# The second branch gate of a hybrid decoder layer as seven half-size products instead of eight projections

## Chip, cores and metric

The kernel runs on 1 core of one Trainium2 chip. The metric is the time of one execution of the whole program on the device, in microseconds (us). Each matrix product is made in fp32r: both operands are split into a high and a low part (`h`, `l`), and a product is three matrix multiplications, h·h + l·h + h·l.

## What is computed

One decoder layer on 512 tokens of 1024 features, in float32:

```python
u = rms_norm(x, g)
z = u @ w_in        # q, k, v | conv q, k | v | output gate | i, f | gate A | gate B
A = moba_attention(...)             # 8 heads of 64
B = mlstm_chunkwise(...)            # 4 heads of 128
merged = sigmoid(ga) * (ya @ w_proj_a) + sigmoid(gb) * (yb @ w_proj_b)
h = x + merged @ w_out
h = h + (silu(g) * up) @ w_down     # g, up = rms_norm(h) @ w_gate_up
return rms_norm(h, norm_final_g)
```

The change is about `gb`, the second branch gate: a product of 512 x 1024 by 1024 x 1024.

## The kernel before

**Units.** The work up to the output projection is a list of weight units (`UNITS`), in the order in which TensorE takes them: q, k, va, ob, vb, qkb, ob, then ga 0 to 7, gb 0 to 7, p 0 to 7 (both branch projections of one block of 128 features) and wo 0 to 7. A unit is 128 x 1024 numbers of weights (512 KB). `load_pair` queues its load on SyncE (SP) into a `raw` tile of the R pool (9 tiles). `split_unit` makes `wh` on ScalarE (ACT) and `wl` on VectorE (DVE), in two tiles of the W pool (10 tiles). The split activations `uh`, `ul` of four feature blocks lie in tiles of these two pools (two in each, named `u` in the trace) until the last unit that reads them, so that 8 tiles of W, four units, are left to the weights. `fill` takes the next unit: it makes the splits up to `LOOK` units ahead, calls `make_sums`, and runs the unit's matrix multiplications.

**Gates.** A unit of ga or gb (`proj`, `run_g`) is 24 matrix multiplications of 128 x 128 by 128 x 512 into one PSUM tile `mm` (there are three): the weights are stationary, the 512 tokens move past. ga is copied out by ACT and scaled by the row `rb` (1/rms of each token) later, in `gate`; gb is scaled by `rb` when DVE moves it out (line 561). `gate(m)` takes the sigmoids; `run_p` multiplies them with the two projections and splits the sum (`mgh`, `mgl`) for wo.

**Steps.** Attention heads and mLSTM heads go through a list of steps; each step calls `fill(1)` once, so that a unit lies between the small products of the heads. In the mLSTM steps each head needs its decay rows `R` (`ml_load`, line 1603: a load of 896 KB on the POOL queue out of `scr`), masked on DVE (line 1615) and taken to Exp on ACT. `ml_d1` and `ml_d2` normalise a head, `ml_e` applies its output gate.

**Sums.** The FFN uses products of sums of weight blocks. `sum_steps` makes these sums (`ws`) in device memory: a copy on the SP queue, then an accumulating DMA on the POOL queue. `make_sums` issues them one by one and lets each wait for a matrix multiplication of the unit before, so that they are spread; they are held back in steps 12 to 20.

**Order.** Each engine and each DMA queue runs its instructions in the order in which they stand. A scheduler makes that order from the program's order and its priorities, within the limits of the pools.

Of the kernel before, what the change touches and what calls it, by code (L numbers as in the profile page):

```python
# [15 lines left out]
P = 128  # L16
# [35 lines left out]

def _unit_order():
# [10 lines left out]
    u += [("gb", m) for m in range(8)]  # L64
    u += [("p", m) for m in range(8)]
# [5 lines left out]
NGEN = len(UNITS)  # L71

# [21 lines left out]
def hybrid_layer_kernel(ctx: ExitStack, tc, xT, wall, wgc, wgu, wds, wdl, g3v, vecs, wgates, consts, rope, out):  # L94
# [71 lines left out]
    def split_hl(src, name="h", dst=None):  # L166

        h, l = dst or (slot(F32R, name + "h"), slot(F32R, name + "l"))
        act_(h, src, AF.Copy)
        V.tensor_tensor(l, src, f(h), op=ALU.subtract)  # L170
        return h, l

# [16 lines left out]
    def load_pair():  # L189
        p = wstate["pair"]  # L190
        if p * 2 >= NU:
            return
        for u in (2 * p, 2 * p + 1):
            raw[u] = blk(name="raw", raw=True)
            nc.sync.dma_start(raw[u], wall[u])
        wstate["pair"] += 1
# [8 lines left out]
    def mm3(ps, wh, wl, wk, rh, rl, start, stop):  # L205

        n = len(wk)
        for j, k in enumerate(wk):
            c = slice(k * P, (k + 1) * P)
            st["mm"] = T.matmul(ps, wh[:, c], rh[j], start=start and j == 0, stop=False)  # L210
            T.matmul(ps, wl[:, c], rh[j], start=False, stop=False)  # L211
# [22 lines left out]
    for k in range(KT):  # L234
        for j in (0, 2) if k == 0 else (0,):
            c = slice(j * P, (j + 2) * P if k == 0 else S)
            nc.sync.dma_start(t0[k // 4][:, k % 4, c], wall[k // 2, :, (k % 2) * S : (k % 2 + 1) * S][:, c])
            if k:
                nc.sync.dma_start(xs[k], xT[k])
    wstate["pair"] = 2  # L240
    wstate["split"] = 4
# [91 lines left out]
    def newton(r, v, new):  # L333
# [3 lines left out]
        V.scalar_tensor_tensor(t, t, -0.5, v, op0=ALU.mult, op1=ALU.mult)  # L337
# [41 lines left out]
    def fill(n=1, mid=None):  # L379

        for _ in range(n):
# [9 lines left out]
            kind, i = UNITS[u]  # L391
# [16 lines left out]
    st = {"made": 0, "hold": False}  # L408
# [156 lines left out]
    for kd in ("ob", "ga", "gb"):  # L565
        run[kd] = run_g(kd)


    mgd = []

    def gate(m):
# [3 lines left out]
        act_(ga, ga, AF.Sigmoid)  # L575
        act_(gb, gb, AF.Sigmoid)

    def run_p(m, wh, wl):
        if m == 0:
            gate(0)  # L580
        if m >= 4:
            load_xr()
        pa, pb = mmb(), mmb()
        mm3(pa, wh, wl, range(4), [t[0] for t in ya], [t[1] for t in ya], True, True)
        mm3(pb, wh, wl, range(4, 8), [t[0] for t in yb], [t[1] for t in yb], True, True)
        yield
        ga, gb = gz.pop(("ga", m)), gz.pop(("gb", m))
        V.tensor_tensor(ga, pa, ga, op=ALU.mult)
        V.tensor_tensor(gb, pb, gb, op=ALU.mult)
        if m < KT - 1:  # L590
            gate(m + 1)
        V.tensor_tensor(ga, ga, gb, op=ALU.add)
        mgd.append(split_hl(ga, "mg"))
# [63 lines left out]
    def run_wo(i, wh, wl):  # L657
# [3 lines left out]
        mm3(ps, wh, wl, range(8), [t[0] for t in mgd], [t[1] for t in mgd], True, True)  # L661
# [54 lines left out]
    def sum_steps():  # L716

        def made(key, *terms):
            t = sums[key] = dram.tile(list(terms[0].shape), F32, name=nm("ws"))
            yield nc.sync.dma_start(t, terms[0], max_dma_last_dim=8192)  # L720
            for x in terms[1:]:
                yield nc.gpsimd.dma_start(t, x, accum_op=ALU.add, max_dma_last_dim=8192)

        for c in range(NG):
            w = wgc[c]
            g = lambda k: sums["gc", c, k]
            yield from made(("gc", c, "S1"), w[0], w[1])
            yield from made(("gc", c, "S3"), w[0], w[2])
            w = wds[c]
            g = lambda k: sums["ds", c, k]  # L730
            yield from made(("ds", c, "S1"), w[1], w[2])
            yield from made(("ds", c, "S3"), w[0], w[1])
# [25 lines left out]
    making = sum_steps()  # L758
# [1112 lines left out]
```

## Time and profile before

| | |
|---|---|
| median of 3 runs | 715.16 us (714.8 to 715.38) |
| the profiled execution | 715.64 us, its span 713.6 us |
| granted TensorE clock, mean of the span | 0.997 |
| PE instructions | 3272 |
| DVE busy, instructions | 600.0 us, 986 |
| ACT busy, instructions | 438.0 us, 746 |
| DMA | 152.69 MB, mean 214 GB/s |

The span runs from the first instruction to the last; 2.04 us of the execution lie around it. The eight units of gb are the ones before the first product of the attention branch's projection (ya), which starts 300.10 us into the span. Where times are given as "at 233 us", they count from the start of the span.

### The profile page before, as it was taken

Reading aid. Unit: us, or ns where it says so; the run is one execution under the profiler, and the core shown is the slowest. Engines: PE = TensorE matmul, PEld = TensorE weight load, DVE = VectorE, ACT = ScalarE, POOL = GpSimd, SP = SyncE. Lnnn points to the kernel's source line nnn. Section 1 sums busy time; section 2 is a strip of 40 time slices with the busy share of each in tenths; the row PEclk is TensorE's granted clock in tenths of the full one; section 3 lists DMA queues with packets and bytes.
Section 4 is the critical chain, followed back from the end, with each engine's and each line's share of the span. In section 5 each row is a group of like instructions: output and inputs, shape, how many; then the busy total and the mean of one; then the engine's idle time right before and its main releaser. Section 6 shows DMA issues by size and latency. Waiting matters only on the chain.

```text
span 713.6 us, 9515 instructions
## 1 busy us (share of the span) xinstructions
PE 703.6 (99%) x3272; PEld 585.8 (82%) x3272; DVE 600.0 (84%) x986; ACT 438.0 (61%) x746; POOL 69.8 (10%) x97
## 2 busy tenths in 40 slices
PE   9999999999999999999999999999999999999995
PEld 6888888887888888888888888888888888888884
DVE  6788977888998578666699887898999799797996
ACT  6634888668784446723354756566675666575665
POOL 0013010000001000000020110011002004003000
PEclk9999999999999999999999999999999999999998
DMA  9759685623159997989988667669569649869703
GB/s 326 290 189 242 207 219 173 199 78 151 60 204 244 277 297 218 275 258 269 265 253 198 218 196 216 233 178 302 198 187 278 226 136 220 312 158 272 217 0 119
DMA packets 47009, 152.69 MB, mean 214 GB/s; under 512 B 5837, under 2 KB 6229, under 8 KB 42481
## 3 DMA queue, kind: packets, MB, share of 16 engines
q1 hardware_dynamic: 36880, 117.33, 47.7%
q0 software_dynamic: 9792, 34.21, 23.5%
q8 instruction: 26, 0.43, 0.2%
q10 hardware_dynamic: 288, 0.56, 0.2%
q14 instruction: 23, 0.18, 0.1%
HBM read 130.00 MB, written 53.52 MB: 257 GB/s over the span
## 4 chain that ended last, share of the span: by engine, by line
PE 82%; DVE 12%; ACT 3%; issue 2%; DVEq 0%; ACTq 0%
PE mm L212 10%; PE mm L210 10%; PE mm L211 10%; PE mm L855 5%; PE mm L856 5%; PE mm L854 5%; PE s L855 3%; PE s L856 3%; PE s L854 3%; PE mm L1104 2%; PE mm L1102 2%; PE mm L1101 2%; PE mm L315 2%; PE acc L315 2%; PE acc L856 1%
## 5 line engine op out<-in xcount | busy, mean ns | idle before, releaser
L157 ACT ACTIVATE w<-raw 128x1024 fp32r<-128x1024 f32 (+2 forms) x107 | 108.1, 1023 | 47.7 <-PE mm L855 20.0
L829 DVE TENSOR_TENSOR w<-raw,w 128x1024 fp32r<-128x1024 f32 x70 | 84.4, 1219 | 21.3 <-ACT w L157 21.0
L157 ACT ACTIVATE wh<-raw 128x1024 fp32r<-128x1024 f32 x56 | 59.0, 1054 | 61.4 <-PE mm L211 58.7
L170 DVE TENSOR_TENSOR wl<-raw,wh 128x1024 fp32r<-128x1024 f32 x56 | 68.2, 1218 | 10.2 <-ACT wh L157 10.0
L854 PE MATMUL mm<-w,bq 128*128 128x512 f32 x160 | 62.2, 389 | 0.0
L855 PE MATMUL mm<-w,bq 128*128 128x512 f32 x160 | 62.2, 389 | 0.0
L856 PE MATMUL mm<-w,bq 128*128 128x512 f32 x160 | 62.2, 389 | 0.0
L210 PE MATMUL mm<-u,wh 128*128 128x512 f32 x128 | 50.3, 393 | 0.0
L211 PE MATMUL mm<-u,wl 128*128 128x512 f32 x128 | 50.0, 391 | 0.0
L212 PE MATMUL mm<-u,wh 128*128 128x512 f32 x128 | 50.0, 390 | 0.0
L212 PE MATMUL mm<-ul,wh 128*128 128x512 f32 x128 | 49.8, 389 | 0.0
L211 PE MATMUL mm<-uh,wl 128*128 128x512 f32 x128 | 49.8, 389 | 0.0
L210 PE MATMUL mm<-uh,wh 128*128 128x512 f32 x128 | 49.8, 389 | 0.0
L854 PEld LDWEIGHTS mm<-w,bq 128*128 128x128 f32 x160 | 30.0, 188 | 6.3
L855 PEld LDWEIGHTS mm<-w,bq 128*128 128x128 f32 x160 | 30.0, 188 | 6.3
L856 PEld LDWEIGHTS mm<-w,bq 128*128 128x128 f32 x160 | 30.0, 188 | 6.2
L1010 DVE TENSOR_TENSOR w<-raw,w 128x1024 fp32r<-128x1024 f32 x25 | 30.2, 1216 | 1.4 <-ACT w L157 1.0
L1102 PE MATMUL mm<-w,ac 128*128 128x512 f32 x80 | 31.2, 389 | 0.0
L1101 PE MATMUL mm<-w,ac 128*128 128x512 f32 x80 | 31.1, 389 | 0.0
L854 PE MATMUL s<-w,bq 128*128 128x512 f32 x80 | 31.1, 389 | 0.0
L855 PE MATMUL s<-w,bq 128*128 128x512 f32 x80 | 31.1, 389 | 0.0
L856 PE MATMUL s<-w,bq 128*128 128x512 f32 x80 | 31.1, 389 | 0.0
(438 smaller groups left out, 1917.1 us busy)
## 6 DMA issues: line engine op xcount, KB each, us to landing
raw<-in_wall_dram SPq DMA_DIRECT2D x56, 512.0 KB, 5.6
raw<-in_wgc_dram SPq DMA_DIRECT2D x30, 512.0 KB, 5.1
raw<-ws SPq DMA_DIRECT2D x30, 512.0 KB, 5.8
ws<-in_wgc_dram SPq DMA_DIRECT2D x10, 1024.0 KB, 6.9
ws<-in_wgc_dram POOLq DMA_DIRECT2D x10, 1024.0 KB, 9.3
raw<-in_wds_dram SPq DMA_DIRECT2D x15, 512.0 KB, 6.6
ws<-in_wds_dram SPq DMA_DIRECT2D x10, 512.0 KB, 7.3
ws<-in_wds_dram POOLq DMA_DIRECT2D x10, 512.0 KB, 6.7
```

Source lines behind the costliest of these rows:

```text
L157: return A.activation(out_, in_, func, **kw)
L170: V.tensor_tensor(l, src, f(h), op=ALU.subtract)
L210: st["mm"] = T.matmul(ps, wh[:, c], rh[j], start=start and j == 0, stop=False)
L211: T.matmul(ps, wl[:, c], rh[j], start=False, stop=False)
L212: T.matmul(ps, wh[:, c], rl[j], start=False, stop=stop and j == n - 1)
L829: V.tensor_tensor(l, t, f(h), op=ALU.subtract)
L854: st["mm"] = T.matmul(ps[t], bh, wh[:, d], start=first and k == 0, stop=False, skip_group_check=not first)
L855: T.matmul(ps[t], bh, wl[:, d], start=False, stop=False, skip_group_check=not first)
L856: T.matmul(ps[t], bl, wh[:, d], start=False, stop=k == 3, skip_group_check=not first)
L1010: V.tensor_tensor(w[k][1], g[k], f(w[k][0]), op=ALU.subtract)
L1101: T.matmul(ps, bh, wh[:, d], start=first and k == 0, stop=False, skip_group_check=not first)
L1102: T.matmul(ps, bl, wh[:, d], start=False, stop=False, skip_group_check=not first)
```

## The change

The gate gb is made as one group `gs` of 14 units (seven weight blocks of 512 x 512, two units each) by a scheme of seven products of half-size blocks in place of eight. The operands change places: the 128 tokens of a block of `u` are stationary and 512 output features move, 12 matrix multiplications of 128 x 128 by 128 x 512 in a unit.

- Four of the seven weight blocks are sums (S1, S2, S3, S4). They are made in device memory as the FFN's sums are, ahead of these: `sum_steps` begins with them, from step 1 of the list that `make_sums` works off; the steps are paced anew by the unit's number, no longer held back in steps 12 to 20, and none is issued during gs.
- The token side needs sums as well. `load_x` loads x anew, in two tiles of 1 MB (`cA`, `cB`) on the POOL queue, and `combine` makes four blocks of them on ACT and DVE (rows of 128 x 256). `recast` splits each block into the half of `uh[0..3]`, `ul[0..3]` that the group before has finished with, 16 splits of 128 x 256.
- The results stand with tokens on the partitions. ACT and DVE move them out and scale them by a token's column (`rt`, `nrt`), DVE turns blocks of 32 x 32 (8 transposes), four DMAs write each half to device memory (`gd`) and four read it back (`gb`), on the POOL queue.
- The projections run in the order 4 to 7, 0 to 3 (`PORD`). The first two leave PSUM by four ACT copies (`pa`, `pb`), and `gate` stands behind these copies; the tiles of gb come in another order of tokens, so that `merge` reads the projection and writes the product with turned access patterns.
- The copy `nsb` of `ml_d1` goes from DVE to ACT, and the scaling by 2^-39 in `ml_d2` goes into the ACT instruction and `newton`, four DVE instructions less.

```diff
+GW = ("W11", "S1", "S2", "W12", "S3", "S4", "W22")
+PORD = (4, 5, 6, 7, 0, 1, 2, 3)
...
-    u += [("gb", m) for m in range(8)]
-    u += [("p", m) for m in range(8)]
+    u += [("gs", i) for i in range(2 * len(GW))]
+    u += [("p", m) for m in PORD]
...
+            if kind == "gs":
+                w, j = GW[i // 2], slice(i % 2 * D, i % 2 * D + D)
+                src = sums["gs", w] if w[0] == "S" else wgb[{"W11": 2, "W12": 3, "W22": 1}[w]]
+                nc.sync.dma_start(raw[u], src[:, j])
...
-            while wstate["split"] <= min(u + LOOK, NGEN - 1):
+            while wstate["split"] <= min(u + LOOK + (kind == "gs"), NGEN - 1):
                 split_unit()
             pos[0] += 1
-            make_sums(st["made"] if st["hold"] else min(st["made"] + 2, 6 * (u - 17) // 7))
+            v = u if u < G0 else max(u + G0, 2 * u - 2 * len(GW)) // 2
+            make_sums(5 * (min(v, G0) - 19 + max(v - G0 - 10, 0)) // 4)
...
+    def load_x():
+        for n, c in (("A", slice(0, 4)), ("B", slice(4, 8))):
+            gs[n] = slot4(name="c" + n)
+            nc.gpsimd.dma_start(gs[n], xT[c].rearrange("k p s -> p k s"))
+        yield
+
+    def combine():
+        for k in range(4):
+            x, v = gs["A"][:, k], gs["B"][:, k]
+            ng = ng1[:, k : k + 1]
+            with tc.issue_after(raw_ins(last["a"])), tc.issue_after(raw_ins(last["v"])):
+                act_(v, v, AF.Copy, scale=col(G1 + k + 4))
+                V.tensor_tensor(x[:, A_], x[:, A_], x[:, B_], op=ALU.subtract)
+            V.scalar_tensor_tensor(x[:, B_], x[:, B_], ng, v[:, B_], op0=ALU.mult, op1=ALU.add)
+            V.scalar_tensor_tensor(v[:, B_], x[:, A_], ng, v[:, B_], op0=ALU.mult, op1=ALU.subtract)
+            V.scalar_tensor_tensor(v[:, A_], v[:, B_], -1.0, v[:, A_], op0=ALU.mult, op1=ALU.subtract)
+            yield
...
+    def run_gs(i, wh, wl):
...
+        for t in range(2):
+            for e in range(2):
+                k = 2 * j + e
+                q = lambda u: u[k0 + k][:, HS * half + P * t : HS * half + P * t + P]
+                c = slice(e * S, (e + 1) * S)
+                g = dict(skip_group_check=not first)
+                st["mm"] = T.matmul(ps[t], q(uh), wh[:, c], start=first and k == 0, stop=False, **g)
+                T.matmul(ps[t], q(uh), wl[:, c], start=False, stop=False, **g)
+                st["gs"] = T.matmul(ps[t], q(ul), wh[:, c], start=False, stop=k == 3, **g)
+        yield
+        if j == 0:
+            if w in ("W11", "S1", "S2", "W12"):
+                recast(w)
+            return
...
+            V.transpose(gs["t", n][:, :, 2 * h + t, :], o.rearrange("p (b e) -> p b e", e=32))
+        if w in ("S4", "W22"):
...
+            for m in range(4):
+                z = gz["gb", 4 * n + m] = slot(name="gb")
+                nc.gpsimd.dma_start(z, d[m * P : (m + 1) * P, :])
...
-        act_(ga, ga, AF.Sigmoid)
-        act_(gb, gb, AF.Sigmoid)
+        with tc.issue_after(raw_ins(last["g"])):
+            act_(ga, ga, AF.Sigmoid)
+            act_(gb, gb, AF.Sigmoid)
...
+        if m in PORD[:2]:
+            q = slot(name="pa"), slot(name="pb")
+            for t, z in zip((pa, pb), q):
+                last["g"] = act_(z, t, AF.Copy)
...
-        V.tensor_copy(nsb, num)
+        act_(nsb, num, AF.Copy)
...
-        V.tensor_scalar(d2, d2, 2.0**-39, None, op0=ALU.mult)
...
-        17: [ml_w(1)], 18: [silu_batch([2, 6, 3, 7])], 19: [ml_w(3)],
+        17: [ml_w(1)], 18: [silu_batch([2, 6, 3, 7])], 19: [ml_w(3)], 20: [load_x()], 25: [combine()],
...
-        st["hold"] = 12 <= n <= 20
```

The order moves in two places of which the prediction speaks. On DVE, before, near the end of the gate; `gb<-mm` moves a finished unit out of PSUM, `wl` is the low part of a weight unit, `nt` and `yb` belong to the mLSTM heads:

```order
L1698 SCALAR_TENSOR_TENSOR nt_2730<-nt_2730,vec,ob_1035 128x512
L170 TENSOR_TENSOR wl_2982<-raw_2814,wh_2981 128x1024
L170 TENSOR_TENSOR yb_2941<-nt_2618,yb_2941 128x512
L561 TENSOR_TENSOR gb_2975<-mm_2950,vec 128x512
L170 TENSOR_TENSOR yb_2941<-nt_2730,yb_2941 128x512
L1698 SCALAR_TENSOR_TENSOR nt_2885<-nt_2885,vec,ob_2120 128x512
L170 TENSOR_TENSOR wl_3024<-raw_2907,wh_3023 128x1024
```

On DVE, now, near the end of gs; `u` is the low part of a recast block, `gW` and `gS` are results on their way out, `gt` the turned ones, and `wl_3101` is the low part of the last unit of gs:

```order
L1852 SCALAR_TENSOR_TENSOR nt_2914<-nt_2914,vec,ob_2247 128x512
L175 TENSOR_TENSOR wl_3039<-raw_2949,wh_3038 128x1024
L658 SCALAR_TENSOR_TENSOR gW_2861<-acc_3011,rt,gW_2861 128x512
L175 TENSOR_TENSOR yb_3000<-nt_2914,yb_3000 128x512
L659 STREAM_TRANSPOSE gt_3054<-gW_2861 128x16x32
L658 SCALAR_TENSOR_TENSOR gW_2863<-acc_3012,rt,gW_2863 128x512
L175 TENSOR_TENSOR wl_3060<-raw_2951,wh_3059 128x1024
L659 STREAM_TRANSPOSE gt_3054<-gW_2863 128x16x32
L175 TENSOR_TENSOR wl_3080<-raw_3007,wh_3079 128x1024
L658 SCALAR_TENSOR_TENSOR gS_2935<-mm_2793,nrt,gS_2935 128x512
L658 SCALAR_TENSOR_TENSOR gS_2937<-mm_2794,nrt,gS_2937 128x512
L659 STREAM_TRANSPOSE gt_3095<-gS_2935 128x16x32
```

Weight units stand twice as close to each other for the same matrix work, and results and transposes stand between them. From the low part of the first unit of the gate to that of the last, DVE had 54 instructions before (8 of 1024 columns, 45 of 512, 1 of 384) and has 98 now (14 of 1024, 50 of 512, 2 of 384, 32 of 256).

On the POOL queue, before, around the decay rows `R`; `ws` are the sums' adding transfers:

```order
L1603 DMA R_1756<-scr 128x1792
L722 DMA ws_1486<-in_wgc_dram 128x2048
L1603 DMA R_2050<-scr 128x1792
L1603 DMA R_2114<-scr 128x1792
L1603 DMA R_2281<-scr 128x1792
L722 DMA ws_2388<-in_wgc_dram 128x2048
L722 DMA ws_2465<-in_wds_dram 64x2048
```

And now, with the gate's sums (`in_wgb`) and x (`cA`, `cB`):

```order
L848 DMA ws_1923<-in_wgb_dram 128x2048
L848 DMA ws_1835<-in_wgc_dram 128x2048
L848 DMA ws_2206<-in_wgb_dram 128x2048
L1758 DMA R_2300<-scr 128x1792
L848 DMA ws_2031<-in_wgc_dram 128x2048
L590 DMA cA_2377<-in_xT_dram 128x4x512
L848 DMA ws_2271<-in_wds_dram 64x2048
L590 DMA cB_2379<-in_xT_dram 128x4x512
L848 DMA ws_2487<-in_wds_dram 64x2048
```

The last head's decay rows now stand behind three adding transfers of 1 MB and ahead of both tiles of x, and `cB` behind one of 0.5 MB more.

More of the change, by code (lines that the diff above doesn't have):

```diff
@@ L71 @@
 NGEN = len(UNITS)
+G0 = UNITS.index(("gs", 0))
 NG = 5
@@ L239, in hybrid_layer_kernel @@
                 nc.sync.dma_start(xs[k], xT[k])
+    wstate["split"] = 4
     wstate["pair"] = 2
-    wstate["split"] = 4
     load_pair()
@@ L406, in proj @@
         return ps
-    st = {"made": 0, "hold": False}
+    st = {"made": 0}
     def run_qk(kind):
@@ L563, in run_g @@
         return fn
-    for kd in ("ob", "ga", "gb"):
+    for kd in ("ob", "ga"):
         run[kd] = run_g(kd)
-    mgd = []
+    A_, B_ = slice(0, HS), slice(HS, S)
+    gs = {}
+    def load_x():
[14 more added lines that the diff above has]
+            yield
@@ L571, in gate @@
+    run["gs"] = run_gs
+    mgd = {}
     def gate(m):
@@ L584, in run_p @@
         mm3(pa, wh, wl, range(4), [t[0] for t in ya], [t[1] for t in ya], True, True)
+        if m == PORD[0]:
+            tc.add_manual_dep(raw_ins(st["first"]), raw_ins(st["gs"]).name, behind, reason="order")
         mm3(pb, wh, wl, range(4, 8), [t[0] for t in yb], [t[1] for t in yb], True, True)
         yield
[L587 to L593, printed above, removed]
+        if m in PORD[:2]:
+            q = slot(name="pa"), slot(name="pb")
+            for t, z in zip((pa, pb), q):
+                last["g"] = act_(z, t, AF.Copy)
+            early.append((m, *q))
+            if m == PORD[1]:
+                gate(PORD[0])
+                for x in early:
+                    merge(*x)
+        else:
+            merge(m, pa, pb)
     run["p"] = run_p
@@ L660, in run_wo @@
         ps = mmb()
-        mm3(ps, wh, wl, range(8), [t[0] for t in mgd], [t[1] for t in mgd], True, True)
+        mm3(ps, wh, wl, range(8), [mgd[k][0] for k in range(KT)], [mgd[k][1] for k in range(KT)], True, True)
         residual()
@@ L716, in sum_steps, with copied, added, groups @@
     def sum_steps():
[L718 to L732, printed above, removed]
+        def copied(a):
+            t = dram.tile(list(a.shape), F32, name=nm("ws"))
+            return t, nc.sync.dma_start(t, a, max_dma_last_dim=8192)
+        def added(key, t, b):
+            i = nc.gpsimd.dma_start(t, b, accum_op=ALU.add, max_dma_last_dim=8192)
+            sums[key] = t
+            return i
+        def groups():
+            prev = None
+            for c in range(NG):
+                w, v = wgc[c], wds[c]
+                for key, a, b in (
+                    (("gc", c, "S1"), w[0], w[1]), (("gc", c, "S3"), w[0], w[2]),
+                    (("ds", c, "S1"), v[1], v[2]), (("ds", c, "S3"), v[0], v[1]),
+                ):
+                    t, i = copied(a)
+                    yield i
+                    if prev:
+                        yield added(*prev)
+                    prev = key, t, b
+            yield added(*prev)
+        rest = groups()
+        s1, i = copied(wgb[0])
+        yield i
+        s3, i = copied(wgb[0])
+        yield i
+        yield added(("gs", "S1"), s1, wgb[1])
+        yield added(("gs", "S3"), s3, wgb[2])
+        yield next(rest)
+        s2, i = copied(s1)
+        yield i
+        yield next(rest)
+        yield added(("gs", "S2"), s2, wgb[2])
+        yield next(rest)
+        s4, i = copied(s2)
+        yield i
+        yield next(rest)
+        yield added(("gs", "S4"), s4, wgb[3])
+        yield from rest
     sums = {}
@@ L1415, in hybrid_layer_kernel @@
     columns(rb[0:1, :], rt.rearrange("p (j h) -> p j h", h=1))
+    ng1 = cst.tile([P, 4], F32, name="ng1")
+    V.tensor_scalar(ng1, vec[:, G1 : G1 + 4], -1.0, None, op0=ALU.mult)
+    nrt = cst.tile([P, 4], F32, name="nrt")
+    V.tensor_scalar(nrt, rt, -1.0, None, op0=ALU.mult)
     man.close()
```

97 lines of the change are left out of this document (78 added, 19 removed).

## The prediction, made before the result was known

> **What bounds the kernel now.** I read the page's busy times first, then PE's waits, then the stretch of the gate engine by engine. The busy times:
>
> ```profile
> PE 703.6 (99%) x3272; PEld 585.8 (82%) x3272; DVE 600.0 (84%) x986; ACT 438.0 (61%) x746; POOL 69.8 (10%) x97
> ```
>
> A busy PE can hide waits, so the view of waits for PE alone decides:
>
> ```profile
> PE s L1571 <- ACT P L162: 1.0, 2, 0.7
> PE s L231 <- DVE mask L219: 1.0, 1, 1.0
> PE acc L1021 <- DVE w L799: 0.6, 1, 0.6
> ```
>
> In the whole span PE waits 2.6 us for others, and nowhere near the gate. PE is the bound from end to end: a matrix multiplication less is time less, and a wait made on PE is time more, one for one. What a multiplication costs is the distance between two starts, not its duration of 0.39. The timeline of PE, first and last row of 90 unbroken ones and the row after:
>
> ```profile
> 279.70 0.39 PE L210 MATMUL mm<-u,wh 128*128 128x512 f32 x1
> ...
> 299.88 0.39 PE L212 MATMUL mm<-ul,wh 128*128 128x512 f32 x1
> 300.10 0.39 PE L210 MATMUL mm<-ya,wh 128*128 128x512 f32 x1
> ```
>
> (300.10 - 279.70) / 90 = 0.2267 us. A unit of ga or gb (24) takes 5.44, one of gs (12) 2.72.
>
> How full are the others there? Windows from the first split of the gate's weights to its end (columns: PE, PEld, DVE, ACT, POOL, clock, DMA share, GB/s):
>
> ```profile
> 233.00:255.00 22.00, 22.00 (x103) 18.38 (x102) 14.64 (x22) 10.75 (x18) 1.62 (x2) 1.00 0.96 269
> 255.00:292.00 37.00, 37.00 (x168) 30.66 (x167) 29.28 (x43) 23.90 (x38) 3.18 (x4) 1.00 0.87 244
> ```
>
> DVE works 43.9 us of 59, ACT 34.7, and the DMA engines are nearly full. The room that the change needs is on DVE and in the DMA.
>
> **Part 1: fewer multiplications.** gb has 8 x 24 = 192, gs 14 x 12 = 168, all of 512 columns, and no other count changes: 24 x 0.2267 = 5.44 us less on the path. This term is certain as long as PE isn't made to wait.
>
> **Part 2: DVE in the gate's stretch.** The distances between starts on DVE, for the widths that matter:
>
> ```profile
> 214.75 1.21 DVE L170 TENSOR_TENSOR wl<-raw,wh 128x1024 fp32r<-128x1024 f32 x1
> 215.88 0.41 DVE L1645 TENSOR_TENSOR R<-R 128x256 f32<-128x256 f32 x1
> 216.22 0.68 DVE L170 TENSOR_TENSOR ya<-ya,ya 128x512 fp32r<-128x512 f32 x1
> 216.82 0.28 DVE L1646 TENSOR_TENSOR R<-R 128x128 f32<-128x128 f32 x1
> 217.02 0.55 DVE L170 TENSOR_TENSOR Al<-R,Ah 128x384 fp32r<-128x384 f32 x1
> 217.49 0.68 DVE L170 TENSOR_TENSOR ya<-ya,ya 128x512 fp32r<-128x512 f32 x1
> ```
>
> 1.13 us for 1024 columns, 0.34 for 256, 0.60 for 512, 0.47 for 384. The transposes I count as 512 columns: the kernel has eight of that size later, a tenth of a microsecond longer at most.
>
> ```profile
> L648 DVE STREAM_TRANSPOSE ht<-xr 128x512 f32<-128x512 f32 x8 | 5.6, 704 | 0.0
> ```
>
> From the first weight unit's low part to the last one's, the 98 instructions of the changed order make 14 x 1.13 + 50 x 0.60 + 2 x 0.47 + 32 x 0.34 = 57.6 us; the 54 of before made 36.5. When may they start? The first split waits for a place in the W pool, four units back, and the places are as many as before:
>
> ```profile
> 232.28 1.06 ACT L157 ACTIVATE wh<-raw 128x1024 fp32r<-128x1024 f32 x1 [5.16 <-PE mm L211]
> 233.38 1.23 DVE L170 TENSOR_TENSOR wl<-raw,wh 128x1024 fp32r<-128x1024 f32 x1 [3.09 <-ACT wh L157]
> ```
>
> So DVE starts at 233.38 and, never idle, ends the last low part at 291.0. Without a stall PE ends gs at 300.10 - 5.44 = 294.66 and starts its last unit at 291.94; that unit's first two products need only the high part, so the low part is due at 292.4. The margin is 1.4 us for everything that DVE waits for in 58. Two kinds of waits come.
>
> (a) x. `combine` stands from the third DVE instruction on, at about 235.6, and needs `cB` and two ACT copies of it (0.5 us each and the hand-over: 1.5). The two tiles go on the POOL queue, among the sums' adds. Its transfers, KB each and median us to landing:
>
> ```profile
> ws<-in_wgc_dram POOLq DMA_DIRECT2D x10, 1024.0 KB, 9.3
> ws<-in_wds_dram POOLq DMA_DIRECT2D x10, 512.0 KB, 6.7
> R<-scr POOLq DMA_DIRECT2D x4, 896.0 KB, 6.2
> h1d<-ht POOLq DMA_DIRECT2D x8, 256.0 KB, 6.1
> ```
>
> The add ahead of `cA` is paced by the second unit of ga, the one ahead of `cB` by the third. The first products of these two on PE before:
>
> ```profile
> 204.26 0.39 PE L210 MATMUL mm<-u,wh 128*128 128x512 f32 x1
> ...
> 211.60 0.44 PE L210 MATMUL mm<-u,wh 128*128 128x512 f32 x1
> ```
>
> 5.44 later, at 209.7 and 217.0, the adds may go. Wholly overlapped, `cB` lands 9.3 after its own issue at about 217.5: 226.8. Wholly one after the other it lands at 209.7 + 9.3 + 9.3 + 6.7 + 9.3 = 244.3. With a DMA share of 0.96 there I take a little past the middle, 236: DVE goes on at 237.5, 1.9 us idle. The Trainium skill would have it otherwise ("DMA: Bandwidth & Descriptors", Anatomy of one DMA): some 2 us and the bytes at 436 GB/s, 4.4 us for 1 MB by its fit; by that the tile is there by 222, this wait is nothing, and the sum below gains 1.9. The rows of this queue (9.3) speak against it in this crowd.
>
> (b) hand-overs. Recast, gates and mLSTM tails go from ACT to DVE and back; such a hop costs about 0.2 us where nothing covers it (0.18 in the row below). I count seven that follow a PE or ACT release late in the order: 1.4.
>
> ```profile
> 267.59 1.23 DVE L170 TENSOR_TENSOR wl<-raw,wh 128x1024 fp32r<-128x1024 f32 x1 [0.18 <-ACT wh L157]
> ```
>
> 1.9 + 1.4 - 1.4 = 1.9 us that PE waits for the low parts of the last units of gs. Bounds: nothing, if `cB` comes before 234; 10, if it comes at 244 (236 gives 1.9, and each microsecond later one more).
>
> **Part 3: ACT, and what is queued behind its waits.** From start to start a split takes 0.95 us there, 512 columns take 0.52 to 0.60:
>
> ```profile
> 204.38 1.05 ACT L157 ACTIVATE wh<-raw 128x1024 fp32r<-128x1024 f32 x1
> 205.33 0.57 ACT L157 ACTIVATE ga<-mm 128x512 f32<-128x512 f32 x1
> 205.93 0.60 ACT L157 ACTIVATE yl<-acc 64x512 f32<-64x512 f32 x1
> ...
> 285.35 0.62 ACT L162 ACTIVATE ga<-ga 128x512 f32<-128x512 f32 x1
> 285.87 0.62 ACT L162 ACTIVATE gb<-gb 128x512 f32<-128x512 f32 x1
> ```
>
> It gains 6 splits, 16 recasts of 256 columns (an estimate of 0.3 each, half of 0.6), 4 copies of x, 6 results and 4 `nsb` (0.55 each): 18 us, together 53 of 59, so it doesn't bind by its sum. But the copies of `cB` stand ahead of the copy that frees the fourth ga unit's PSUM, which the seventh wants at about 240.6: PE is hit there directly if `cB` comes after 238. At 236 it costs nothing. Likewise the last decay rows:
>
> ```profile
> 209.95 1.14 DVE L1615 SCALAR_TENSOR_TENSOR R<-con,cS,R 128x128 f32<-128x128 f32 x4 [0.90 <-DMA R<-scr]
> ```
>
> DVE waits 0.9 us for them already. Now up to one more add of 9.3 us lies ahead of them; I take 3 us, which the 3.09 us of idle time in the row at 233.38 swallows. If that cover is gone it adds to (a).
>
> **Part 4: the way back of gb.** The first half is complete when S4 has left PE, 5.44 us ahead of the end of gs. DVE evacuates and turns it behind low parts that are due first (about 6 us after PE), the four stores take 0.68 x 3 + 6.1 = 8.1 (issues follow each other at 0.68, row below), the loads 5 to 7 (the 256 KB row above), then a sigmoid, three more ACT instructions and a sum on DVE, 4.4, until the third projection's first product leaves PSUM.
>
> ```profile
> 367.85 2.66 POOL L652 DMA_DIRECT2D h1d<-ht  x4 [6.90 <-DVE v L687]
> ```
>
> 6 + 8.1 + 6 + 4.4 = 24.5. PE wants that PSUM tile 5.44 + 3 x 5.44 + 2.72 = 24.5 us after S4. It is a tie, which part 2's delay of PE loosens a little; I take 0.5 (0 to 3). The second half has 10 us more. ACT stands with the sigmoid until then; the weight splits behind it are four units early, so only this PSUM tile counts.
>
> **Nothing else on the path.** The sums' 8 MB run mostly between 125 and 214, and the loads of gs are seven units early. The DMA engines' busy tenths, 40 slices of 17.8 us:
>
> ```profile
> DMA  9759685623159997989988667669569649869703
> ```
>
> Slices 8 to 12, from 125 on, are 6, 2, 3, 1 and 5: there is room. `nsb` and the four scalings are counted above. For wo the last projection now comes fourth of eight, not last. How long its way out of PSUM and its split take, from the seventh of before, which leaves PE at 300.10 + 7 x 5.44 = 338.2:
>
> ```profile
> 338.38 0.69 DVE L589 TENSOR_TENSOR gb<-mm,gb 128x512 f32<-128x512 f32 x1 [1.69 <-PE mm L212]
> ...
> 340.85 0.68 DVE L170 TENSOR_TENSOR mgl<-ga,mgh 128x512 fp32r<-128x512 f32 x1
> ```
>
> 3.3 us to the end of the low part. The order puts five products of the next unit ahead of the one that needs it, and reaches that after 15 products, 3.4 us; 0.1. FFN, tail and start keep their order but for pacing.
>
> **Sum.** -5.44 + 1.9 + 0.5 + 0.1 = -2.9 us. The profiled execution took 715.64 (span 713.6 and 2.04 around it), which makes 712.7; against the median of the runs, 715.16, it is 712.2. That is 0.4% faster. 0.2% (1.43 us) is about what a measurement of this kernel can tell from no change.
>
> **The rivals.**
>
> No stall (chance 0.2): the transfers overlap well, `cB` lands before 234 and the hops hide. Then all of 5.44 stays: 709.7. For it: PE's clean record, and splits that are four units early. Against it: 57.6 us in a room of 59.
>
> The return of gb is late (0.15): a load beside two streams needs 9 us in place of 6, and PE waits 3 us ahead of the fourth projection's second product. -5.44 + 1.9 + 3.0 + 0.1 = -0.4: 714.7, no change. For it: the POOL queue's 8 transfers one behind the other. Against it: no sum is issued then.
>
> x is late (0.15), the one that ends slower: each microsecond after 234 is one of DVE's lateness, and so of PE's. It decides from 240.5 on (5.44 + 1.43 - 0.6 = 6.3 us lost). At 242 the sum is -5.44 + 7.9 + 0.5 + 0.1 = +3.1: 718.3. For it: DMA shares of 0.96, and four MB on one queue between 209 and 235. Against it: two transfers usually overlap.
>
> That the change doesn't do what it says is out: the order has the 24 multiplications less.
>
> **How the numbers follow.** The forecast has 0.5, the rivals 0.2, 0.15 and 0.15. The range reaches from no stall, 709.6, to 716.0, where x is 5.7 us late; it leaves out the last rival. Faster by over 0.2% are the first, nearly all of the forecast and a little of the third case: 0.70; no change 0.15; slower 0.15.
>
> **What would show it.** Right: 24 PE instructions less at the same distance; PE's waits near the end of gs name DVE `wl`, some 2 us; DVE idle ahead of L600 to L602 names ACT `cB`, and behind that the DMA. Part 4 is wrong if PE waits nowhere between gs and wo, or for several microseconds. All is wrong if PE waits in ga already, if the FFN's loads of `ws` come late for their new pacing, or if the distance of 0.2267 grows with weights as the moving operand.

## The result

| | before | after |
|---|---|---|
| median | 715.27 us (4 runs, 714.80 to 715.74) | 722.38 us (4 runs, 721.74 to 723.08) |
| profiled execution, its span | 715.64, 713.6 us | 721.74, 720.0 us |

The ratio is 1.010, with a 95% interval of 1.0082 to 1.0117: the change costs 7.1 us where 2.9 us of gain were forecast. The profile after is of the fastest of its four runs; the sums below are made against its span. PE has the 24 instructions less:

```profile
PE 702.3 (98%) x3248; PEld 582.7 (81%) x3248; DVE 617.6 (86%) x1024; ACT 460.5 (64%) x788; POOL 84.4 (12%) x119
```

5.44 us less on PE and a span longer by 6.4 mean 11.8 us that PE lost. The waits of PE in after that before doesn't have:

```profile
PE s L1834 <- DVE d L1837: 4.5, 1, 4.5
PE mm L223 <- DVE ga L689: 2.2, 1, 2.2
...
PE mm L1252 <- ACT w L162: 0.5, 1, 0.5
PE mm L223 <- ACT ga L162: 0.4, 1, 0.4
```

The first is the norm sum of the last mLSTM head (head 3, counted from 0), inside gs. Its place in the timeline of PE, and that of the second wait:

```profile
266.24 0.39 PE L634 MATMUL s<-wl,u 128*128 128x512 f32 x1
271.14 0.77 PE L1834 MATMUL s<-sqh,onesr 128*128 128x512 f32 x1 [4.51 <-DVE d L1837]
271.71 0.63 PE L1835 MATMUL s<-sql,onesr 128*128 128x512 f32 x1
...
275.97 0.48 PE L635 MATMUL mm<-wh,u 128*128 128x512 f32 x1
276.29 0.40 PE L633 MATMUL mm<-wh,u 128*128 128x512 f32 x1
...
321.66 0.39 PE L227 MATMUL mm<-ya,wh 128*128 128x512 f32 x1
324.26 0.50 PE L223 MATMUL mm<-yb,wh 128*128 128x512 f32 x1 [2.21 <-DVE ga L689]
```

Gaps are given here and below as distances of starts, less the 0.227 that a multiplication takes: 4.67 us in the first. Behind it twelve starts take 276.29 - 271.14 = 5.15 in place of 12 x 0.2267 = 2.72: 2.43 more. The window of that stretch shows why (columns as in the prediction):

```profile
271.00:276.30 5.30, 5.16 (x13) 4.08 (x14) 4.29 (x7) 3.57 (x6) 0.00 (x0) 0.51 0.62 198
```

The granted clock is 0.51 there. The second gap costs 2.37, with no slow stretch behind it. With the two small waits (0.5 and 0.7 between starts) that is 10.6 of the 11.8; the rest lies in pieces that I did not follow.

Where the first gap comes from, the chain that ended last tells, in order of time:

```profile
227.64 11.62 DMA cB<-in_xT_dram
239.42 0.50 issue
239.92 0.52 ACT Ah L162
...
270.40 0.61 DVE d L1837
271.14 0.77 PE s L1834
```

x's second half sets it. The rows of POOL, ACT and DVE at its ends:

```profile
227.64 0.81 POOL L590 DMA_DIRECT2D cB<-in_xT_dram  x1 [9.40 <-PE s L1791]
...
239.29 0.72 ACT L162 ACTIVATE cB<-cB,vec 128x512 f32<-128x512 f32 x1 [5.58 <-DMA cB<-in_xT_dram]
...
240.46 0.56 DVE L175 TENSOR_TENSOR Al<-R,Ah 128x384 fp32r<-128x384 f32 x1 [5.49 <-ACT Ah L162]
```

POOL had nothing to do for 9.4 us: the load waited for L1791, the score products of the last mLSTM head, whose q and k lie in the large tile that `cB` takes over (the four heads' score products start near 172, 189, 203 and 219; the last of them starts at 227.06). It landed at 239.26. ACT stood in front of it for 5.6 us with the splits `Ah` queued behind, and DVE stood for 5.5 us on `Ah`. From then to 271 DVE has not a tenth of a microsecond to make that up. The rows of head 2's norm sum on PE and of its read on DVE:

```profile
265.11 0.39 PE L1835 MATMUL s<-sql,onesr 128*128 128x512 f32 x1
270.32 0.68 DVE L1837 SCALAR_TENSOR_TENSOR d<-d,s 128x512 f32<-128x512 f32 x1
```

PE left that sum at 265.3, DVE reads it 5 us later. Until it is read, PE can't write head 3's: S has three PSUM tiles, and gs holds two of them from 262 on.

### The profile page after: what moved, and what is told of

Read it like the earlier page. It is cut to its first block, busy times and chain, and to the rows that moved or that the text cites. A ratio compares the mean times of both kernels' runs of the same rounds, so it can differ in the third digit from the quotient of the medians.

```text
span 720.0 us, 9618 instructions
## 1 busy us (share of the span) xinstructions
PE 702.3 (98%) x3248; PEld 582.7 (81%) x3248; DVE 617.6 (86%) x1024; ACT 460.5 (64%) x788; POOL 84.4 (12%) x119
## 4 chain that ended last, share of the span: by engine, by line
PE 71%; DVE 17%; ACT 5%; issue 4%; DMA 2%; DVEq 0%; ACTq 0%
PE mm L223 6%; PE mm L227 6%; PE mm L226 5%; PE mm L1009 5%; PE mm L1008 5%; PE mm L1007 5%; PE s L1009 3%; PE s L1008 3%; PE s L1007 3%; PE mm L1252 2%; PE mm L1255 2%; PE mm L1253 2%; DVE wl L175 2%; PE mm L330 2%; DMA cB<-in_xT_dram 2%
## 5 line engine op out<-in xcount | busy, mean ns | idle before, releaser
L175 DVE TENSOR_TENSOR wl<-raw,wh 128x1024 fp32r<-128x1024 f32 x62 | 75.0, 1216 | 13.3 <-ACT wh L162 12.5
L162 ACT ACTIVATE wh<-raw 128x1024 fp32r<-128x1024 f32 x62 | 65.2, 1055 | 31.8 <-PE mm L226 20.5
L223 PE MATMUL mm<-u,wh 128*128 128x512 f32 x96 | 37.9, 395 | 0.4 <-ACT ga L162 0.4
L227 PE MATMUL mm<-u,wh 128*128 128x512 f32 x96 | 37.5, 391 | 0.0
L226 PE MATMUL mm<-u,wl 128*128 128x512 f32 x96 | 37.5, 390 | 0.0
L227 PE MATMUL mm<-ul,wh 128*128 128x512 f32 x96 | 37.4, 389 | 0.0
L223 PE MATMUL mm<-uh,wh 128*128 128x512 f32 x96 | 37.4, 389 | 0.0
L226 PE MATMUL mm<-uh,wl 128*128 128x512 f32 x96 | 37.3, 389 | 0.0
```

The source lines that it names most:

```text
L162: return A.activation(out_, in_, func, **kw)
L175: last["v"] = V.tensor_tensor(l, src, f(h), op=ALU.subtract)
L227: T.matmul(ps, wh[:, c], rl[j], start=False, stop=stop and j == n - 1)
```

## The experiments

All but the two on gaps were timed beside the kernel before on the same chip; after was timed at another time, and the median of before lay between 715.03 and 715.41 us in all of these. Rows and windows are of one profiled execution each; in the first three runs below it is the longest (721.97, 719.66 and 721.81 us).

**What makes the gap at 266.** First, the last head's norm sum gets a tile of its own.

```diff
     def ml_d2(h, sqn, d2, nsb):
-        ps = sb()
+        ps = accb() if h == 3 else sb()
```

> The last head's norm sum (L1834, L1835 of head 3) goes into a tile of acc instead of S; nothing else changes. Theory: after loses 4.67 us in front of that sum, and about 2.2 us more because the matrix multiplications behind the gap run 0.43 apart instead of 0.227; the gap exists because two of the three S tiles belong to the gate from 262 on, so heads 2 and 3 share one, and DVE, 5.5 us late through cB, reads it late. With a tile of its own head 3 waits for nobody: the gap and the slow stretch go, 722.4 - 6.9 = 715.5. Rival: DVE has simply too much to do, and its lateness comes out at the next place where PE needs it (the low parts of the recast x or of the weights); then 718 or more, with PE's waits naming DVE wl or u.

Measured 721.28 us, 1.1 less than after. The gap is gone, and its time came back in pieces:

```profile
PE mm L223 <- DVE ga L689: 2.8, 1, 2.8
PE acc L1835 <- DVE sql L175: 1.5, 1, 1.5
...
PE mm L634 <- DVE wl L175: 1.1, 1, 1.1
...
PE s L634 <- DVE wl L175: 0.8, 2, 0.4
```

The rival is right: the shared tile is only the first place where DVE's lateness meets PE. Second, the combination starts a step later, so that nobody stands in front of `cB`.

```diff
-20: [load_x()], 25: [combine()],
+20: [load_x()], 26: [combine()],
```

> The combination of x starts one step of the mLSTM loop later (26 instead of 25), so that nothing of ACT or DVE is queued behind the wait for cB; the S tiles stay as they are. Theory: DVE doesn't stand idle for 5.5 us at 235 to 240, reads head 2's norm sum at about 265 to 267 instead of 270.3, and the gap before head 3's sum shrinks to 0 to 1.5 us, too short for the slow stretch; the 0.6 at 240.8 (PE waiting for ACT's copy of ga) goes too: 715 to 717. Rival (DVE's amount of work is the cause, not its idle time): PE still waits over 3 us there, 719 or more.

Measured 717.28 us, 5.1 less than after and just above the range that was expected. No gap at 266; what is left in gs are waits for `wl`, where the prediction had put them, and the wait for gb is longer:

```profile
PE mm L223 <- DVE ga L689: 4.0, 1, 4.0
...
PE s L634 <- DVE wl L175: 1.0, 2, 0.6
```

Third, the cause of the cause: is it the tile that makes `cB` late, or the crowd?

```diff
-            gs[n] = slot4(name="c" + n)
-            nc.gpsimd.dma_start(gs[n], xT[c].rearrange("k p s -> p k s"))
+            if n == "A":
+                gs[n] = slot4(name="cA")
+                nc.gpsimd.dma_start(gs[n], xT[c].rearrange("k p s -> p k s"))
+            else:
+                gs[n] = [slot(name="cB") for _ in range(4)]
+                for k in range(4):
+                    nc.gpsimd.dma_start(gs[n][k], xT[4 + k])
...
```

> The changed kernel with one edit: cB lies in four tiles of 128x512 from the pool of single tiles instead of one large tile, so its load doesn't wait for the large tile that the second head's q and k leave at 227; it goes out right behind cA, the combination stays at step 25. Theory: it is the tile that makes cB late (issued at 227.6, landed at 239.3, DVE idle 5.5); with cB landed by 232 or so nobody waits for it, the gap of 4.7 at 266 with its slow stretch and the 0.6 at 240.8 go, and as in the run with the later combination PE stands some 4 us for the way back instead: 717 (716 to 718). Rival: the crowd on the DMA engines makes it late whichever tile it has (landed after 236): 720 or more.

Measured 717.79 us, no gap at 266, 3.4 us before the fourth projection. The later combination isn't needed then. But the edit does two things: the load no longer waits for the large tile, and each copy of ACT now needs only a quarter of `cB`. The second half of the load, and ACT's first copies:

```profile
L595 POOL DMA_DIRECT2D cB<-in_xT_dram x2: 556/557/558, 218.4 to 218.9; - x2
DMA to landing us min/median/max: 18.2/18.6/19.0
...
235.37 1.33 ACT L162 ACTIVATE cB<-cB,vec 128x512 f32<-128x512 f32 x2
```

The quarters landed at 229.5, 231.0, 236.6 and 237.9. The last one was issued 8.7 us earlier than the whole tile in after and came only 1.3 us earlier, so for the second half the rival, the crowd on the DMA engines (share 1.02 from 226 to 240), is right. ACT waited for none of them, since its first two copies need only the first half. So some 5 of the 7 us come from ACT and DVE standing in front of `cB`, which two runs show; how much of that is the tile's doing and how much the crowd's isn't shown, as no run loads `cB` in one piece into a free tile.

**The way back of gb.** One more projection without a gate:

```diff
-        if m in PORD[:2]:
+        if m in PORD[:3]:
...
-            if m == PORD[1]:
+            if m == PORD[2]:
```

> The third projection too is copied out of PSUM by ACT before its gate is there (PORD[:3] instead of PORD[:2]). Theory: the wait of 2.4 us at 321.7 (PE for DVE ga L689) is only the way back of gb, and one more projection of 5.44 us without a gate covers it: 722.4 - 2.4 = 720.0. Rival: DVE then has three merges to make up, and PE waits for PSUM at the fifth or sixth projection instead: 721.5 to 723.

Measured 719.17 us, 3.2 less than after; PE waits 0.8 us one projection later. And on top of the later combination, no way back at all (the gate's second branch is made of weights instead of gb):

```diff
-            d = dram.tile([S, S], F32, name=nm("gd"))
-            for q in range(4):
...
-                nc.gpsimd.dma_start(z, d[m * P : (m + 1) * P, :])
+                nc.gpsimd.dma_start(z, wgb[n][:, m * S : (m + 1) * S])
```

> The combination one step later, and gb doesn't go through DRAM: its eight tiles are loaded from weights, the stores are left out, so the gates are not the reference's; all else stays. Theory: with DVE on time PE stands 4.1 us before the fourth projection only for the way back of gb, and another 1.75 for the slow stretch behind that gap: 717.3 - 5.9 = 711.4. Rival: the sigmoids, merges and splits that stand in a queue there take as long without it: 714 or more.

Measured 714.09 us (ratio to before 0.9982, 0.9973 to 0.9991). PE waits nowhere between gs and wo, so the way back is what it waited for. The spans, 711.9 against 717.9 with the way back, differ by the 6 us that were expected, but the latter is of the longest run. The medians differ by 3.2, and 711.4 wasn't reached. The eight runs go from 715.78 to 719.66: four with a mean granted clock of 0.994 or 0.995 from 717.65 up, four with 0.996 to 0.998 below 717. It seems that not all of them have the slow stretch behind the gap; only one was profiled. A fourth early projection, beside the three edits (next part):

```diff
-        if m in PORD[:3]:
+        if m in PORD[:4]:
...
-            if m == PORD[2]:
+            if m == PORD[3]:
```

> The three edits, and a fourth projection copied out of PSUM ahead of its gate. Theory: the 0.93 us (1.3 with what follows) that PE waits before the fifth projection, for DVE's merges, is covered: 715.1 - 1.2 = 713.9. Rival: the merges are only queued up longer, and PE waits as long one projection later: 715.

Measured 721.36 us, worse by 6.3. The rival, and more than it had: the sigmoids stand behind ACT's last copy, and DVE's merges behind them, four at a time, while PE wants the PSUM tile of the fifth projection.

```profile
PE mm L223 <- DVE ga L689: 4.9, 1, 4.9
```

**The three edits together** (norm sum in acc, combination at 26, three early projections).

> The three edits together. Theory: everything that after lost against a PE that never waits is these: 722.4 - 6.9 (gap and slow stretch) - 0.6 (ga) - 2.4 (gb) = 712.5, 2.8 less than before, range 711.5 to 713.5. Rival (DVE too full for the seven products): not below 715.3, the time of before.

Measured 715.07 us beside 715.03 of before, ratio 0.9999 (0.9991 to 1.0008). They give back 7.3 us, not 9.9; the rival's bound, the time of before, holds. What PE still waits for:

```profile
PE s L634 <- DVE wl L175: 1.0, 2, 0.6
...
PE mm L634 <- DVE wl L175: 0.9, 1, 0.9
PE mm L223 <- DVE ga L689: 0.8, 1, 0.8
```

Is that DVE's amount of work? Leave the combination of x out (x goes into the products as loaded):

```diff
         for k in range(4):
-            x, v = gs["A"][:, k], gs["B"][:, k]
...
             yield
```

> The three edits, and the combination of x is left out: x goes into the seven products as it was loaded, so the gate's second branch is not the reference's; 16 DVE instructions of 0.34 (5.4 us) and 4 ACT copies are gone. Theory: the amount of DVE's work is what is left; the waits for wl (2.45) go, DVE is ahead, and gb is back earlier (0.9): 715.1 - 3.4 = 711.7. Rival: hand-overs from ACT, not DVE's amount, set the low parts' time: 714 or more.

Measured 713.04 us, 2.0 less where 3.4 were expected (ratio to before 0.9967, 0.9955 to 0.9980). No wait for `wl` of any size is left, so it is this work that makes them; the edit takes four ACT copies and the need for x away as well, and no run parts these from the 5.4 us of DVE instructions. The 0.8 before the fifth projection stays, it is DVE's merges there. Four tries to keep the combination and spare DVE. The products with the low part last:

```diff
-                T.matmul(ps[t], q(uh), wl[:, c], start=False, stop=False, **g)
-                st["gs"] = T.matmul(ps[t], q(ul), wh[:, c], start=False, stop=k == 3, **g)
+                T.matmul(ps[t], q(ul), wh[:, c], start=False, stop=False, **g)
+        for t in range(2):
+            for e in range(2):
...
+                st["gs"] = T.matmul(ps[t], q(uh), wl[:, c], start=False, stop=k == 3, **g)
```

> The three edits, and in a unit of gs the four products with the weights' low part come last instead of second of three. Theory: what is left of DVE's lateness in the run with the three edits is three waits for wl (1.09, 0.57 and 0.79 us), each because the low part is needed 0.23 us after a unit's start; now it is needed 8 x 0.2267 = 1.8 us after, and the waits are gone. Part of it may come back before the fifth projection, where PE waits 0.9 for the way back of gb: 715.1 - 2 = 713.1 (712.5 to 714.3). Rival: DVE is full without a pause, so each low part comes later still, and the waits only move on to later units: 714.7 or more.

Measured 716.17 us: the waits only move (1.3 us for DVE's evacuation `gS` instead of `wl`). Work given to POOL (a sign goes into the split of that block):

```diff
-                V.tensor_tensor(x[:, A_], x[:, A_], x[:, B_], op=ALU.subtract)
+                nc.gpsimd.tensor_tensor(x[:, A_], x[:, A_], x[:, B_], op=ALU.subtract)
...
-            V.scalar_tensor_tensor(v[:, A_], v[:, B_], -1.0, v[:, A_], op0=ALU.mult, op1=ALU.subtract)
+            nc.gpsimd.tensor_tensor(v[:, A_], v[:, A_], v[:, B_], op=ALU.add)
...
-        V.tensor_tensor(ga, ga, rb, op=ALU.mult)
+        nc.gpsimd.tensor_tensor(ga, ga, rb, op=ALU.mult)
```

> The three edits, and two kinds of work go from DVE to POOL, which has little to do there: of the combination of x the two steps that are a plain difference or sum (8 instructions of 0.34), and the scaling of ga ahead of its sigmoid (8 of 0.60, of which 5 lie between 236 and 262). Theory: DVE's amount of work in the stretch is the bound; with about 5.7 us less, the waits for wl (2.45, with what follows them 3.1) go: 715.1 - 2.8 = 712.3. The output stays the reference's. Rival: DVE's own instructions become longer while POOL computes, or POOL's queue makes them wait: 715 or more.

Measured 716.19 us. The rival, and its rows, one of POOL and two of DVE:

```profile
241.19 1.09 POOL L682 TENSOR_TENSOR ga<-ga,vec 128x512 f32<-128x512 f32 x1 [3.91 <-ACT ga L162]
...
241.31 2.05 DVE L175 TENSOR_TENSOR wl<-raw,wh 128x1024 fp32r<-128x1024 f32 x1
...
248.13 1.22 DVE L175 TENSOR_TENSOR wl<-raw,wh 128x1024 fp32r<-128x1024 f32 x1
```

A low part of the same shape takes 2.05 us while POOL computes and 1.22 when it doesn't. With the fourth early projection beside it:

> The work given to POOL and the fourth early projection together. Theory: both gains add up: 715.1 - 2.8 - 1.2 = 711.1, 4 us less than before. Rival: as in the two runs beside it; not below 714.

Measured 722.34 us; both fail together as they do alone. Work that isn't due held back, behind the last transposition of the gate (`last["t"]`):

```diff
-        V.tensor_tensor(ga, ga, rb, op=ALU.mult)
+        with tc.issue_after(raw_ins(last["t"])):
+            V.tensor_tensor(ga, ga, rb, op=ALU.mult)
```

> The three edits, and DVE's scaling of ga (8 instructions of 0.60, not due before the sigmoids) is held behind the last transposition of the gate; in the run with the three edits 7 of them stood between 226 and 262, ahead of low parts that are due, and DVE was idle for 7.8 us between 305 and 314. Theory: DVE's queue from 240 to 292 is the bound, 4.2 us less in it take the waits for wl away: 715.1 - 2.7 = 712.4. Rival: those scalings stood in pauses of DVE (1.8 to 2.1 us idle at 238), so nothing comes of it: 714.7 or more; or they now delay the merges, and PE waits longer before the fifth projection.

Measured 715.63 us. The rival: those scalings had stood in pauses. From 226 to 254 DVE now works 21.5 us in place of 23.8 with the three edits, and from 254 to 292 37.9 of 38 in both. One of the pauses:

```profile
253.99 0.69 DVE L1838 SCALAR_TENSOR_TENSOR d<-d,s 128x512 f32<-128x512 f32 x1 [0.73 <-PE s L1836]
```

On top of it a copy of the fourth projection's first product, and then the low parts last as well:

```diff
+            if m == PORD[3]:
+                z = slot(name="pa")
+                act_(z, pa, AF.Copy)
+                pa = z
             merge(m, pa, pb)
```

> As the run beside it, and of the fourth projection only the first product (pa) is copied out of PSUM by ACT, so that DVE's merges of the first three no longer stand between it and the fifth projection's PSUM tile. Theory: the wait of 0.93 (1.3 with what follows) goes: 712.4 - 1.2 = 711.2. Rival: ACT's copy stands behind sigmoids and comes no earlier than DVE's merge: 712.4.

> As the run beside it, and the products with the weights' low part last in each unit of gs. Theory: with a DVE that isn't full without a pause, 1.8 us of slack cover what waits for wl are left: 711.0. Rival: nothing left to cover, 711.2 as without it; or, as in the first run with this order, the end of a product comes later and DVE's evacuation with it: 712 or more.

Measured 715.74 and 716.28 us: the wait before the fifth projection is 0.8 as before, now for the second product's tile (DVE gb L693), so ACT's copy doesn't help while that one stays. Last, the combination earlier, in own tiles and with the other two edits, at step 25 and at 24 (the tiles as in the diff above).

> As the run beside it, with the last head's norm sum in a tile of acc and three early projections. Theory: the combination is done some 10 us earlier than in the run with the three edits, in the stretch in which DVE has pauses, so up to 5 us of work are gone from the stretch in which it is full, as in the run without the combination: 713.0, with the reference's output. Rival: DVE is full from about 240 on in any order, 715.1 as with the three edits.

> As the run beside it, and the combination starts a step earlier (24). Theory: if cB has landed by 230, more of the combination falls into DVE's pauses: 712.5. Rival: cB isn't there yet, ACT and DVE stand for it, and the gap of after comes back in part: 716 or more.

Measured 716.04 and 715.63 us, where 713.0 and 712.5 were expected. Windows of the first of the two, with DVE's busy time in the third place:

```profile
240.00:254.00 14.00, 14.00 (x67) 11.72 (x66) 11.59 (x24) 8.30 (x17) 1.65 (x2) 1.00 0.82 233
254.00:266.00 12.00, 12.00 (x56) 9.58 (x55) 12.00 (x19) 11.81 (x22) 0.00 (x0) 1.00 0.91 236
266.00:276.00 10.00, 10.00 (x46) 8.18 (x45) 10.00 (x18) 9.89 (x18) 0.00 (x0) 1.00 0.41 139
276.00:292.00 16.00, 14.05 (x60) 10.53 (x59) 16.00 (x25) 11.73 (x19) 0.00 (x0) 1.00 0.36 109
```

DVE works 38 of 38 us from 254 to 292. From 226 to 254 it works 23.8, as with the three edits: the combination comes earlier, but other work comes later, with 2.4 us of pauses between 240 and 254. So, it seems, only work that lies behind 254 counts, and none of the versions that keep the output takes enough of it away. None of those beats the kernel before.

**The slow stretch by itself.** The kernel before, with four gaps made ahead of the odd projections: ACT copies in a chain, which the projection waits for; then the same with shorter ones.

```diff
+        if m % 2:
+            z = slot(name="dum")
+            hold = act_(z, f(ya[0][0]), AF.Copy)
...
+            for _ in range({1: 3, 3: 4, 5: 5, 7: 8}[m]):
+                hold = act_(z, z, AF.Copy)
...
+            tc.add_manual_dep(raw_ins(st["head"]), raw_ins(hold).name, after, reason="gap")
```

> The kernel before, and four gaps made on PE: ahead of the projections 1, 3, 5 and 7 a chain of 4, 5, 6 and 9 ACT copies of 512 columns (about 0.6 us each) starts when the unit before has nearly left PE, and the projection waits for its end: gaps of about 2.1, 2.7, 3.3 and 5 us. Theory: behind a gap of 2.4 us the matrix multiplications run on at 0.227, behind one of 2.9 or more about 9 of them run 0.43 apart and 1.7 to 2.2 us are lost on top; so the first gap costs only itself, the last two cost 2 us more each, the second lies at the edge: 715.2 + 13.1 + 4 to 6 = 732 to 735. Rival: the slow stretch belongs to the place (many loads and other engines at work), not to the gap: no slow stretch here, 728.

> The kernel before with four shorter gaps on PE: projection 1 waits for ACT's split of the projection before (mgh), 3 for one ACT copy more, 5 for DVE's low part (mgl), 7 for two ACT copies more; by the run with the long gaps (4.84 with 4 copies, 0.66 for each) that is about 2.2, 2.9, 2.7 and 3.5 us. Theory: the slow stretch starts where a gap is longer than somewhere between 2.4 (none) and 2.96 (one): none behind the first, one behind the last, with 1.4 to 2.2 us lost. Rival: any gap of 1 us or more has one: all four.

The chains started later than I had thought, behind ACT's split of the projection before: gaps of 4.83, 5.49, 6.16 and 8.14 us, 747.5 us. Behind each of them the clock is halved at once. The timeline of PE behind the first:

```profile
310.56 0.80 PE L210 MATMUL mm<-ya,wh 128*128 128x512 f32 x1 [4.68 <-ACT dum L157]
311.15 0.63 PE L213 MATMUL mm<-ya,wl 128*128 128x512 f32 x1
...
313.59 0.40 PE L213 MATMUL mm<-ya,wl 128*128 128x512 f32 x1
```

Seven starts in 3.03 us in place of 1.59: 1.4 lost. In the run with short gaps, 730.3 us:

```profile
308.08 0.50 PE L210 MATMUL mm<-ya,wh 128*128 128x512 f32 x1 [2.17 <-ACT mgh L157]
...
322.00 0.50 PE L210 MATMUL mm<-ya,wh 128*128 128x512 f32 x1 [2.75 <-ACT dum L157]
...
336.45 0.50 PE L210 MATMUL mm<-ya,wh 128*128 128x512 f32 x1 [3.25 <-DVE mgl L605]
...
350.97 0.50 PE L210 MATMUL mm<-ya,wh 128*128 128x512 f32 x1 [3.35 <-ACT dum L157]
...
351.77 0.61 PE L210 MATMUL mm<-ya,wh 128*128 128x512 f32 x1
352.18 0.63 PE L213 MATMUL mm<-ya,wl 128*128 128x512 f32 x1
```

Only the last, of 3.51 us between starts, has a slow stretch, from 0.8 us behind its end; those of 2.90 and 3.41 have none, so the bound that was expected, between 2.4 and 2.96, isn't it. Slow stretches come in the kernel before too where long gaps are made: the gap makes them, not the place.

## Why the prediction was wrong

**Part 1, 5.44 us less: right.** 24 instructions less, and with weights as the moving operand they start as far apart as before.

**Part 2, 1.9 us for x and hand-overs: this is the step that failed.** Three things in it. The landing of `cB` was worked out from the adds ahead of it on its queue and the transfers' durations, and taken at 236 (226.8 to 244.3). It landed at 239.3, inside the bounds, but for another reason: the step never asked which tile `cB` takes and who still reads it. The queue was idle for 9.4 us; the tile held the load. Its transfer then took 11.6 us beside others (DMA share 1.01 from 226 to 240) and not 9.3. By the fit of the Trainium skill quoted in the prediction ("DMA: Bandwidth & Descriptors", Anatomy of one DMA) 1 MB would take 4.4 us, an estimate that this crowd contradicts. Without the wait for the tile, in four pieces, the last quarter landed at 237.9, so the crowd alone makes it later than 236 too. By the prediction's own price, 1 us of PE's for each after 234, 239.3 makes 5.2 us in place of 1.9; PE lost 7.1, and at another place. With nobody standing in front of `cB` (the later combination) 5.1 us come back. Then, DVE's 98 instructions were given one due date, the last low part at 292.4, with a margin of 1.4. They have many, and the first of DVE's that PE missed is the read of head 2's norm sum at 266, because gs takes two of the three S tiles; the prediction never names these tiles. The run with a tile more shows that the place matters little and the lateness much. And a wait of PE was priced "one for one", where 4.67 cost 7.1 with the halved clock behind it.

DVE's amount of work was sized nearly right: with the three edits it goes from the first low part at 232.77 to the start of the last at 293.25, 57.5 us of work and 2.96 of waits, where the sum has 56.5 up to there. PE then waits for `wl` near the end of gs, 1.9 us (1.2 in the run with the later combination). That this is the 1.9 of the forecast is luck: with no wait for x, the prediction's own sum, 1.4 of hand-overs less a margin of 1.4, leaves nothing. What stood in its place are two waits of DVE for products of the mLSTM heads, 2.10 and 0.86 us, which had been counted at 0.2 each or not at all.

**Part 3: right.** PE was to be hit at 240.6 if `cB` came after 238; it came at 239.3, and PE waits 0.4 for ACT's copy of ga (0.5 between starts). The wait for the last decay rows grew from 0.9 to 5.2 us on DVE (3 more had been taken) and met PE nowhere, as said.

**Part 4, 0.5 us (0 to 3): the mechanism right, the size wrong.** The last product of S4 starts at 297.18. These rows of DVE and POOL follow it; the last is of the chain, which goes on with the load:

```profile
302.29 1.29 DVE L659 STREAM_TRANSPOSE gt<-gS 128x512 f32<-128x512 f32 x2
...
303.87 2.65 POOL L663 DMA_DIRECT2D gd<-gt  x4 [49.29 <-DVE gt L659]
315.26 2.17 POOL L669 DMA_DIRECT2D gb<-gd  x4 [8.73 <-ACT pb L162]
...
315.26 3.83 DMA gb<-gd
```

Out of PSUM and turned: 6.2 (6 forecast). From the first store to the loads' issue: 11.4 (8.1). Load: 3.8 (6). From there to PE at 324.26: 5.2 (4.4). With 0.3 to the first store that makes 26.9 in place of 24.5, and PE waits the difference, 2.4. The stores are the mis-sized term: they were priced at 6.1, the median of eight stores of the same size and row length that took 5.1 to 8.6, and the four took 6.5, 7.3, 7.9 and 8.7, each longer than the one before. The view names ACT's copy `pb` as what the load waited for; in other runs it names other instructions there, but in after and four runs beside it the load is issued 0.6 to 0.7 us behind the last of these landings. As soon as PE is earlier this wait grows (4.0 with the later combination), so "part 2's delay of PE loosens it" was right, and also the reason why mending one of the two gains less than its wait.

**The rest.** FFN was said to be unchanged but for pacing; a new wait of 0.5 at 475 belongs to it. The price of wo's order was not followed.

**The rivals.** "x late" was the mechanism, with its place in the queue and not in the tile, and its price at 239.3 would have been 0.4 us over before. "gb late" came as well, near its number (2.4 for 3.0) but not by its mechanism: the first load took 3.8 us, not 9, and the stores were late. They were given 0.15 each and summed one without the other, but nothing keeps them apart, and both came. A range that let them add up (-5.44 + 5.2 + 3.0 + 0.1 = +2.9) would have reached to 718; of the 4 us beyond that, 2.4 are the clock.

## What to carry to other kernels

Of a load that is moved, ask for its tile first: the queue may be empty, and the load still stands until the last reader of the tile's former tenant is done, with everything queued behind the first who needs it. Ask for the traffic beside it too: here a free tile brought the last quarter only 1.3 us earlier. Of an engine that is to be filled to 97%, list every due date on the way (PSUM tiles that others wait for, ways through memory), not the last one: lateness comes out at the first and, mended there, at the next. Price a wait of the bounding engine with what its clock does afterwards.

## What the runs showed of the hardware

- **A gap halves TensorE's clock for a while.** In after and in the two runs with gaps, gaps of 2.33, 2.37, 2.90 and 3.41 us between starts left the spacing at 0.227; those of 3.51, 4.67 and all longer ones were followed by starts 0.43 apart, 1.4 to 2.7 us lost. The Trainium skill ("TensorE: Matmul & The Clock Gate", What's actually happening) has free-running windows of some 3.4 us, one idle one of which halves the clock; by their lengths these gaps agree, though the slow stretch behind the one of 3.51 begins only 0.8 us after PE has started again. Two runs don't agree: with the norm sum in acc a gap of 2.96 us, and with cB in own tiles one of 3.39, were followed by a slow stretch too, both behind several shorter gaps in the 55 us ahead; the first began 1.1 us behind the gap's end. Why is open.

```profile
322.90 0.50 PE L223 MATMUL mm<-yb,wh 128*128 128x512 f32 x1 [2.80 <-DVE ga L689]
...
324.00 0.63 PE L226 MATMUL mm<-yb,wl 128*128 128x512 f32 x1
324.43 0.63 PE L227 MATMUL mm<-yb,wh 128*128 128x512 f32 x1
```

- **POOL's computing holds DVE up.** 2.05 us in place of 1.22 beside a POOL instruction of 1.09. The Trainium skill ("SBUF — State Buffer", SBUF: two separate sides) has the two share a pair of ports under an exclusive lock, which a DVE instruction with two inputs in SBUF also needs; the low parts are such, and the rows agree: held until POOL ends at 242.28 and then 1.22 us long, the low part would end at 243.50, and it ends at 243.36.
